# Shared rows turned on TensorE and stored as eight rows, early reloads into other places, one root for a norm of four tiles

## The chip, the cores and the metric

The kernel runs on one core of a Trainium2 chip. The metric is the device time of one execution in microseconds (us). The engines of the core are TensorE (PE, matrix products), VectorE (DVE), ScalarE (ACT), GpSimd (POOL) and SyncE (SP, which here only issues transfers); each takes its own instructions in order, and they wait for one another by semaphores. Transfers between DRAM and the on-chip memory are issued from a queue of SP or of POOL and run on 16 DMA engines.

## The reference

One layer on 1024 tokens of width 1024, all in float32:

```python
mod = silu(c) @ w_ada + b_ada
sh1, sc1, g1, sh2, sc2, g2 = split(mod, 6)
h = x * (1 + sc1) + sh1
z = h @ w_in + b_in
y = concat([y_a, y_b, y_c, y_d]) @ w_o        # four causal mixers on slices of z
x = layer_norm(ALPHA * x + (1 + g1) * y, ln1_g, ln1_b)
h = x * (1 + sc2) + sh2
f = (silu(h @ w_gate) * (h @ w_up)) @ w_down
x = layer_norm(ALPHA * x + (1 + g2) * f, ln2_g, ln2_b)
```

`mod` has six parts of 1024 numbers that are the same for every token. Two of them, `1 + g1` and `1 + g2`, multiply along the width of a tile whose rows are tokens, so each of the 128 partitions needs all 1024 numbers: a shared row.

## The kernel before

A float32 product is made of three products of pairs: `split` (L79) casts a tile to a high part on ACT (L80) and takes the low part as a difference on DVE (L81), and `passes` (L128) issues three matmuls, L130 to L132, into one PSUM bank. So every operand that PE reads has been through one ACT and one DVE instruction first.

Weights arrive through SP's queue in tiles of 128x1024, 512 KB each, in a ring of four buffers, `raw` (L71): a load waits in the queue until the tile that held its buffer has been read for the last time, and everything behind it in the queue waits too. `ada(j)` (L166) multiplies a tile of `w_ada` with the condition on DVE (L168) and so gives one column of `mod`: 128 numbers, one per partition; eight such columns are one part. There are 48 of them, spread over the first half of the program and a part of the second.

`spread` (L469) makes a shared row: it stores the eight columns to DRAM (L472) and loads the 1024 numbers back into all 128 partitions (L474). It is called twice, for `g1row`, which `res1` (L573) reads, and for `g2row`, read by `res2` (L849).

The tokens are in two halves, c = 0 and c = 1, of four tiles of 128. The program runs: input projections and mixers; the output projection of half 0, tile by tile in five steps (`first_step`, `tail`), with the y of the last mixer, the short convolution, finished on DVE in `short_out` (L877); `ln1` of half 0, which also stores the transposed h2 to DRAM; gate and up products of half 0 (`c11`); output projection and `ln1` of half 1 (`out_proj1`, `done`), interleaved with more `c11`; then the gate and up products of the other quarters after Strassen's scheme (`strassen`), for which `ln1` of half 1 makes the sum operands T1: L613 loads half 0's first four k-tiles of h2 back (`b11`), L614 subtracts, L618 stores the result; then the down-projection, also by Strassen (`dn_product`), in which each quarter's operands come by loads L810 and go through `split`. It ends with the last norms, `ln2` (L855). Half 1's norms stand in the middle of the last products, half 0's at the very end.

`ln2` works by tile: statistics of two half rows (L861, L863), their aggregate (L864), a root on POOL (`rsqrt`, L390, nine small instructions L397 to L415 for one column, twelve for four), then two passes over the row (L867, L871) and a store for each half row (L872). `ln1_[t]` is the generator of tile t of half 1; `run` advances it by one or all its steps, and the steps' places among the products set the order on DVE, as the code is written.

The order of the instructions on PE, and in parts on DVE and ACT, is that of the code (`in_order`); elsewhere a scheduler places them. An `after(a, b)` sets an issue order between two instructions.

## Time and profile before

| | |
|---|---|
| time, three runs | median 1024.22 us (1017.43 to 1025.0) |
| the profiled execution | 1024.31 us, its span 1022.5 us |
| granted TensorE clock, mean | 0.974 |
| PE busy | 960.3 us, 94% |
| DVE busy | 807.9 us, 79% |
| ACT, POOL busy | 358.0 us and 200.1 us |
| moved | 197.93 MB, mean 194 GB/s |

The span runs from the first instruction to the last. All positions in the profile are us from the span's start. The granted clock is a share of full speed: 1.00 is 2.4 GHz, 0.50 is 1.2 GHz. A bracket at the end of a timeline row tells how long the engine had been idle before that instruction, and what it waited for.

### The profile page before, as it was taken

The numbers are of one execution on the slowest core, as the hardware profiler recorded it, in microseconds if no ns is written. First come the engines' busy times: TensorE is split into PE (matmuls) and PEld (weight loads), VectorE is DVE, ScalarE is ACT, GpSimd is POOL, SyncE is SP. The second block draws the span as 40 slices with busy tenths as digits, with TensorE's granted clock in tenths as the row PEclk, the third lists the DMA queues.
The fourth block names the chain that finished last, engine by engine and source line by source line (L and its number), as shares of the span: only waits on it lengthen the run. The fifth ranks groups of instructions, "written<-read, shape, count | busy, mean of one in ns | idle before, by whom it ended". The sixth has DMA issues, their size and how long they took to land.

```text
span 1022.5 us, 12397 instructions
## 1 busy us (share of the span) xinstructions
PE 960.3 (94%) x4348; PEld 779.2 (76%) x4348; DVE 807.9 (79%) x1268; ACT 358.0 (35%) x545; POOL 200.1 (20%) x537
## 2 busy tenths in 40 slices
PE   8949999898999999988989999999999999999984
PEld 7737777676887877877768788888788877888863
DVE  5848998789669963638798888888766799898887
ACT  4532221342473353275332222222223243544230
POOL 7990000300251020352000000000000000000506
PEclk9979999999999999999999999999999999999998
DMA  8923212786554464378965554445438897655542
GB/s 310 322 99 127 58 34 71 246 206 232 177 190 175 144 224 147 128 276 265 339 238 216 196 195 168 167 180 158 163 133 272 308 308 267 216 192 176 189 150 82
DMA packets 78751, 197.93 MB, mean 194 GB/s; under 512 B 11425, under 2 KB 17601, under 8 KB 78689
## 3 DMA queue, kind: packets, MB, share of 16 engines
q1 hardware_dynamic: 67648, 157.82, 46.5%
q0 software_dynamic: 11040, 39.33, 10.6%
q8 instruction: 34, 0.56, 0.2%
q14 instruction: 29, 0.23, 0.1%
HBM read 153.79 MB, written 42.74 MB: 192 GB/s over the span
## 4 chain that ended last, share of the span: by engine, by line
PE 29%; issue 26%; DVE 11%; POOL 8%; DMA 7%; ACT 3%; SPq 0%; POOLq 0%; DVEq 0%; ACTq 0%
PE mm L132 9%; PE mm L130 9%; PE mm L131 9%; DVE pr L81 3%; DMA tmp<-in_w_down_dram 2%; DVE acc L429 1%; DMA raw<-in_w_ada_dram 1%; DVE raw L168 1%; POOL rs_b L402 1%; ACT tmp L603 1%; POOL rs_a L397 1%; DMA raw<-h_d 1%; ACT pr L80 1%; PE sm L130 1%; DMA raw<-in_w_o_dram 1%
## 5 line engine op out<-in xcount | busy, mean ns | idle before, releaser
L80 ACT CAST pr<-raw 128x1024 fp32r<-128x1024 f32 (+1 forms) x157 | 133.6, 876 | 178.5 <-PE mm L132 67.8
L81 DVE TENSOR_TENSOR pr<-raw,pr 128x1024 fp32r<-128x1024 f32 (+1 forms) x157 | 155.3, 1002 | 32.9 <-ACT pr L80 32.4
L130 PE MATMUL mm<-bop,pr 128*128 128x512 f32 x264 | 103.4, 392 | 2.5 <-DVE c L774 1.5
L132 PE MATMUL mm<-bop,pr 128*128 128x512 f32 x264 | 102.8, 389 | 0.0
L131 PE MATMUL mm<-bop,pr 128*128 128x512 f32 x264 | 102.7, 389 | 0.0
L131 PE MATMUL mm<-pr 128*128 128x512 f32 x250 | 97.9, 391 | 4.7 <-DVE pr L81 4.7
L130 PE MATMUL mm<-pr 128*128 128x512 f32 x250 | 97.4, 390 | 0.1
L132 PE MATMUL mm<-pr 128*128 128x512 f32 x250 | 97.3, 389 | 0.0
L429 DVE SCALAR_TENSOR_TENSOR acc<-up,pack,acc 128x512 f32<-128x512 f32 x120 | 84.6, 749 | 0.1
L130 PE MATMUL mm<-h,pr 128*128 128x512 f32 (+1 forms) x208 | 78.2, 376 | 6.5 <-ACT p L650 5.6
L132 PE MATMUL mm<-h,pr 128*128 128x512 f32 (+1 forms) x208 | 76.4, 367 | 2.9 <-DVE pr L81 2.9
L131 PE MATMUL mm<-h,pr 128*128 128x512 f32 (+1 forms) x208 | 76.6, 368 | 0.0
L130 PE MATMUL mm<-tb,pr 128*128 128x512 f32 x176 | 69.5, 395 | 2.9 <-DVE tmp L764 2.9
L132 PE MATMUL mm<-tb,pr 128*128 128x512 f32 x176 | 69.6, 396 | 0.7 <-DVE pr L81 0.7
L131 PE MATMUL mm<-tb,pr 128*128 128x512 f32 x176 | 69.0, 392 | 0.0
L168 DVE SCALAR_TENSOR_TENSOR raw<-raw,cond 128x1024 f32<-128x1024 f32 x48 | 58.0, 1220 | 13.2 <-DMA raw<-in_w_ada_dram 13.1
L397 POOL TENSOR_SCALAR rs_a<-lmv 128x1 f32<-128x1 f32 x16 | 9.2, 575 | 295.2 <-DVE lmv L864 179.5
L80 ACT CAST pr<-room 128x512 fp32r<-128x512 f32 x60 | 34.3, 618 | 86.8 <-PE mm L132 83.1
L130 PEld LDWEIGHTS mm<-bop,pr 128*128 128x128 f32 x264 | 49.5, 188 | 15.4 <-issue 2.1
L131 PEld LDWEIGHTS mm<-pr 128*128 128x128 f32 x250 | 46.9, 188 | 16.2 <-DVE pr L81 6.7
L132 PEld LDWEIGHTS mm<-bop,pr 128*128 128x128 f32 x264 | 49.6, 188 | 10.4
L131 PEld LDWEIGHTS mm<-bop,pr 128*128 128x128 f32 x264 | 49.6, 188 | 9.9
(337 smaller groups left out, 2153.9 us busy)
## 6 DMA issues: line engine op xcount, KB each, us to landing
raw<-in_w_ada_dram SPq DMA_DIRECT2D x48, 512.0 KB, 4.9
raw<-in_w_down_dram SPq DMA_DIRECT2D x25, 512.0 KB, 3.4
raw<-in_w_gate_dram SPq DMA_DIRECT2D x23, 512.0 KB, 4.8
raw<-in_w_up_dram SPq DMA_DIRECT2D x23, 512.0 KB, 4.3
raw<-s_d SPq DMA_DIRECT2D x20, 512.0 KB, 4.9
raw<-in_w_o_dram SPq DMA_DIRECT2D x16, 512.0 KB, 4.7
raw<-act_d SPq DMA_DIRECT2D x15, 512.0 KB, 4.1
tmp<-in_w_down_dram SPq DMA_DIRECT2D x15, 512.0 KB, 4.6
```

The lines of the kernel that those rows point to most:

```text
L80: S.copy(hi, src)
L81: V.tensor_tensor(out=lo, in0=src, in1=hi.bitcast(F32), op=SUB)
L130: PE.matmul(o, wh, xh, start=first, stop=False, skip_group_check=True)
L131: PE.matmul(o, wh, xl, start=False, stop=False, skip_group_check=True)
L132: PE.matmul(o, wl, xh, start=False, stop=last, skip_group_check=True)
L168: V.scalar_tensor_tensor(out=w, in0=w, scalar=1.0, in1=cond, op0=MUL, op1=MUL, accum_out=mod[:, j:j + 1])
L397: G.tensor_scalar(out=a, in0=v, scalar1=EPS, scalar2=None, op0=ADD)
L402: G.tensor_scalar(out=b, in0=o, scalar1=o, scalar2=a, op0=MUL, op1=MUL)
L429: V.scalar_tensor_tensor(out=o, in0=u, scalar=dww[:, i, j:j + 1], in1=o, op0=MUL, op1=ADD)
L603: S.activation(dst, src, AF.Identity, scale=hA[:, kk:kk + 1], bias=hB[:, kk:kk + 1])
```

## The change

1. `spread` turns the eight columns on PE: `PE.transpose` gives an 8x128 block in PSUM, ACT copies it into the first eight partitions of the row tile, and the store writes 8 runs of 128 numbers instead of 1024 single numbers. The call for `g1row` moves from before `ada(34)` to after `first_step(0)`.
2. `b11` gets its own places, half of the second row tile (tag "rowb") twice and the two accumulators of the convolution, and its four loads are written before `out_proj1` instead of inside `ln1`.
3. For half 1 a new generator, `ln2_all`, takes the four tiles together: all statistics, one root of 128x4, both passes on whole rows, and stores of whole rows at its end, of which the one of tile 0 is ordered behind the last load.

```diff
     def spread(col, tag):
         row_d = dr.tile([1, D], F32, name=f"{tag}_d", bufs=2)
-        SP.dma_start(row_d.rearrange("o (k p) -> (o p) k", p=P), col)
+        o = sm()
+        PE.transpose(o[:KT, :P], col, ident)
         row = yp.tile([P, D], F32, name="row", tag=tag)
+        turned = row[:KT, :P]
+        S.copy(turned, o[:KT, :P])
+        SP.dma_start(row_d.rearrange("o (k p) -> (o k) p", p=P), turned)
         SP.dma_start(row, row_d.to_broadcast([P, D]))
...
         if c == 1:
-            b11 = raw_p.tile([P, 1024], F32, name="raw", tag="raw", bufs=4)
-            bv = b11[:, :CH].rearrange("p (k t) -> p k t", k=4)
-            SP.dma_start(bv, h2_d[:4, :, t * P:(t + 1) * P].rearrange("k p t -> p k t"))
+            bv = b11[t]
             V.tensor_tensor(out=bv, in0=hv[:, :4], in1=bv, op=SUB)
...
+    def ln2_all(rr):
+        st = cst.tile([P, 4, 2, 6], F32, name="lst4")
+        mv = cst.tile([P, 4, 2], F32, name="lmv4")
+        rs = cst.tile([P, 4], F32, name="lrs4")
+        for h in (1, 0):
+            for t, r in enumerate(rr):
+                V.bn_stats(st[:, t, h], r[:, H[h]])
+            yield
+        for t in range(4):
+            V.bn_aggr(mv[:, t], st[:, t])
+        rsqrt(rs, mv[:, :, 1])
+        yield
+        for t, r in enumerate(rr):
+            V.scalar_tensor_tensor(out=r, in0=r, scalar=mv[:, t, 0:1], in1=l2g, op0=SUB, op1=MUL)
+            V.scalar_tensor_tensor(out=r, in0=r, scalar=rs[:, t:t + 1], in1=l2b, op0=MUL, op1=ADD)
+            yield
+        for t, r in enumerate(rr):
+            i = SP.dma_start(out[(4 + t) * P:(5 + t) * P], r)
+            if t == 0:
+                after(i, loaded[-1])
...
-        g1row = spread(mod[:, 16:24], "rowa")
         for j in range(34, 40):
             ada(j)
...
             first_step(n)
+            if n == 0:
+                g1row = spread(mod[:, 16:24], "rowa")
             ada(24 + 2 * n)
...
+        b11 = yp.tile([P, 2, CH], F32, name="b11", tag="rowb")
+        b11 = [b11[:, t] for t in range(2)] + [sl.tile([P, CH], F32, name="b11", tag=f"acc{i}") for i in range(2)]
+        b11 = [b.rearrange("p (k t) -> p k t", k=4) for b in b11]
+        for t in range(4):
+            SP.dma_start(b11[t], h2_d[:4, :, t * P:(t + 1) * P].rearrange("k p t -> p k t"))
         out_proj1(mid, done)
...
-            run(ln1_[t], 1)
+        run(ln1_, 1)
...
-        for t in range(2):
-            run(ln1_[t])
+        run(ln1_, 2)
...
-            if g in (1, 3):
-                run(ln1_[2 + g // 2])
+            if g < 4:
+                run(ln1_, 1)
+        run(ln1_)
```

The order on SP around the first shared row (`rowa_d` is its copy in DRAM, `row` its tile). Before:

```order
L73 DMA raw<-in_w_ada_dram 128x1024 x2
L472 DMA rowa_d<-mod 128x8x1
L73 DMA raw<-in_w_ada_dram 128x1024 x6
L474 DMA row<-rowa_d 128x1024
L73 DMA raw<-in_w_ada_dram 128x1024 x4
L73 DMA raw<-in_w_o_dram 128x1024
L73 DMA raw<-in_w_ada_dram 128x1024 x4
L73 DMA raw<-in_w_o_dram 128x1024 x5
```

With the change:

```order
L73 DMA raw<-in_w_ada_dram 128x1024 x12
L73 DMA raw<-in_w_o_dram 128x1024
L73 DMA raw<-in_w_ada_dram 128x1024 x4
L73 DMA raw<-in_w_o_dram 128x1024
L477 DMA rowa_d<-row 8x128
L73 DMA raw<-in_w_o_dram 128x1024 x2
L478 DMA row<-rowa_d 128x1024
L73 DMA raw<-in_w_o_dram 128x1024 x2
```

The store and the row load have moved behind all those w_ada loads and now stand among the five w_o loads.

On SP around `ln1` of half 1 (L613 loads `b11`, L757 belongs to the Strassen products). Before:

```order
L757 DMA p_4017<-p_d 128x1024
L613 DMA raw<-h_d 128x4x128 x2
L73 DMA raw<-in_w_gate_dram 128x1024
L73 DMA raw<-in_w_up_dram 128x1024
L613 DMA raw<-h_d 128x4x128 x2
L73 DMA raw<-in_w_gate_dram 128x1024
L73 DMA raw<-in_w_up_dram 128x1024
```

With the change, first where the loads of `b11` now stand, some 25 rows of the queue earlier (their tiles are called `b`), then the place they have left:

```order
L1065 DMA b_3281<-h_d 128x4x128
L73 DMA raw<-in_w_gate_dram 128x1024
L73 DMA raw<-in_w_up_dram 128x1024
L1065 DMA b_3281<-h_d 128x4x128
...
L1065 DMA b_3282<-h_d 128x4x128
L1065 DMA b_3283<-h_d 128x4x128
...
L759 DMA p_4019<-p_d 128x1024
L73 DMA raw<-in_w_gate_dram 128x1024
L73 DMA raw<-in_w_up_dram 128x1024
L73 DMA raw<-in_w_gate_dram 128x1024
```

The weights of the next products now follow the `p` load directly.

On DVE in the last norm of half 1, where `r` are its rows, `lmv` the means, `lrs` the roots and `pr` operands for PE. Before:

```order
L867 SCALAR_TENSOR_TENSOR r_6274<-r_6274,lmv,row 128x1024
L864 BN_AGGR lmv<-lst_7360 128x2
L871 SCALAR_TENSOR_TENSOR r_6274<-r_6274,lrs,row 128x512 x2
L81 TENSOR_TENSOR pr<-raw,pr 128x512
L867 SCALAR_TENSOR_TENSOR r_6275<-r_6275,lmv,row 128x1024
L81 TENSOR_TENSOR pr<-raw,pr 128x1024
L871 SCALAR_TENSOR_TENSOR r_6275<-r_6275,lrs,row 128x512 x2
L864 BN_AGGR lmv<-lst_7366 128x2
L867 SCALAR_TENSOR_TENSOR r_6276<-r_6276,lmv,row 128x1024
L871 SCALAR_TENSOR_TENSOR r_6276<-r_6276,lrs,row 128x512
L81 TENSOR_TENSOR pr<-raw,pr 128x1024 x2
L871 SCALAR_TENSOR_TENSOR r_6276<-r_6276,lrs,row 128x512
```

With the change:

```order
L891 SCALAR_TENSOR_TENSOR r_6279<-r_6279,lmv_7360,row 128x1024
L81 TENSOR_TENSOR pr<-raw,pr 128x1024
L81 TENSOR_TENSOR pr<-raw,pr 128x512
L892 SCALAR_TENSOR_TENSOR r_6278<-r_6278,lrs_7361,row 128x1024
L892 SCALAR_TENSOR_TENSOR r_6279<-r_6279,lrs_7361,row 128x1024
L891 SCALAR_TENSOR_TENSOR r_6280<-r_6280,lmv_7360,row 128x1024
L81 TENSOR_TENSOR pr<-raw,pr 128x512
L81 TENSOR_TENSOR pr<-raw,pr 128x1024
L892 SCALAR_TENSOR_TENSOR r_6280<-r_6280,lrs_7361,row 128x1024
L891 SCALAR_TENSOR_TENSOR r_6281<-r_6281,lmv_7360,row 128x1024
L892 SCALAR_TENSOR_TENSOR r_6281<-r_6281,lrs_7361,row 128x1024
L81 TENSOR_TENSOR pr<-raw,pr 128x1024 x2
```

The four aggregates (L887) now stand just ahead of these rows, and each reader of a root (L892, in place of L871) reads a column of the one wide root, `lrs`.

## Rows read from the trace of the kernel before

**Rows 1.** The page: busy us (share of the span) and instructions of each engine.

```profile
PE 960.3 (94%) x4348; PEld 779.2 (76%) x4348; DVE 807.9 (79%) x1268; ACT 358.0 (35%) x545; POOL 200.1 (20%) x537
```

**Rows 2.** Windows: A:B, length, busy PE, PEld, DVE, ACT, POOL, clock, DMA share, GB/s.

```profile
217.76:241.43 23.67, 20.37 (x87) 15.80 (x85) 23.67 (x47) 5.83 (x10) 0.00 (x0) 1.00 0.77 268
241.96:245.37 3.41, 3.41 (x10) 2.66 (x9) 3.41 (x5) 0.00 (x0) 0.00 (x0) 0.50 0.65 238
463.82:467.24 3.42, 3.42 (x9) 2.66 (x9) 3.29 (x6) 0.00 (x0) 0.55 (x1) 0.50 0.98 385
500.00:525.00 25.00, 21.20 (x82) 15.52 (x81) 22.62 (x37) 9.38 (x15) 2.15 (x4) 0.94 0.97 365
```

**Rows 3.** PE's timeline: start, length, line, operands; in brackets idle time before, releaser.

```profile
241.49 0.50 PE L130 MATMUL mm<-pr,ys 128*128 128x512 f32 x1 [3.20 <-DVE y L877]
463.07 0.50 PE L130 MATMUL mm<-h,pr 128*128 128x512 f32 x1 [2.72 <-ACT p L650]
717.99 0.47 PE L130 MATMUL mm<-tb,pr 128*128 128x512 f32 x1 [0.69 <-DVE tmp L764]
976.15 0.50 PE L131 MATMUL mm<-pr 128*128 128x512 f32 x1 [2.15 <-DVE pr L81]
990.04 0.50 PE L131 MATMUL mm<-pr 128*128 128x512 f32 x1 [0.94 <-DVE pr L81]
993.56 0.40 PE L130 MATMUL mm<-pr 128*128 128x512 f32 x1
```

**Rows 4.** DVE's timeline, same columns.

```profile
217.76 1.23 DVE L168 SCALAR_TENSOR_TENSOR raw<-raw,cond 128x1024 f32<-128x1024 f32 x1 [3.67 <-DMA raw<-in_w_ada_dram]
456.17 0.69 DVE L614 TENSOR_TENSOR raw<-tmp,raw 128x512 f32<-128x512 f32 x1 [8.58 <-DMA raw<-h_d]
806.30 1.23 DVE L1091 TENSOR_TENSOR keep<-tmp 128x1024 f32<-128x1024 f32 x1 [5.62 <-DMA tmp<-in_w_down_dram]
809.18 0.69 DVE L1088 TENSOR_SCALAR keep<-keep 128x1024 f32<-128x1024 f32 x1
974.21 0.75 DVE L871 SCALAR_TENSOR_TENSOR r<-r,lrs,row 128x512 f32<-128x512 f32 x1 [2.73 <-POOL lrs L415]
974.88 2.35 DVE L81 TENSOR_TENSOR pr<-raw,pr 128x1024 fp32r<-128x1024 f32 x2
995.98 0.67 DVE L1132 TENSOR_TENSOR f<-mm,row 128x512 f32<-128x512 f32 x1
```

**Rows 5.** SP's queue: start of issuing, time from first to last issue, transfer, count.

```profile
203.44 0.38 SPq L472 DMA_DIRECT2D rowa_d<-mod  x1
204.75 16.46 SPq L73 DMA_DIRECT2D raw<-in_w_ada_dram  x6
244.34 6.64 SPq L73 DMA_DIRECT2D raw<-in_w_o_dram  x5
451.63 1.37 SPq L613 DMA_DIRECT2D raw<-h_d  x2
800.72 0.50 SPq L1087 DMA_DIRECT2D keep<-in_ln_b_row_dram  x1
```

**Rows 6.** The page, transfers: count, size, median us from issue to landing.

```profile
raw<-in_w_ada_dram SPq DMA_DIRECT2D x48, 512.0 KB, 4.9
```

**Rows 7.** The row stores of L472, both.

```profile
DMA to landing us min/median/max: 8.9/9.7/10.5
```

**Rows 8.** The loads of b11, L613, all four.

```profile
DMA to landing us min/median/max: 2.9/3.8/4.7
```

**Rows 9.** POOL's timeline: a wide root, the t_d store, one instruction of a small root.

```profile
365.23 1.10 POOL L397 TENSOR_SCALAR rs_a<-cmv 128x4 f32<-128x4 f32 x1 [0.87 <-DVE cmv L451]
369.26 0.20 POOL L415 TENSOR_TENSOR crs<-crs,rs_b 128x4 f32<-128x4 f32 x1
446.19 0.76 POOL L618 DMA_DIRECT2D t_d<-raw  x1
958.51 1.17 POOL L402 TENSOR_SCALAR rs_b<-lrs,rs_a 128x1 f32<-128x1 f32 x1
```

More of the change, by code (lines that the diff above doesn't have):

```diff
@@ L799, in strassen @@
         G.dma_start(s_d[j, 1].rearrange("p a t -> p (a t)"), hi[1])
+    loaded = []
     GR = tuple((j, min(j + 2, FT // 2)) for j in range(0, FT // 2, 2))
@@ L809, in rows @@
             t = raw_p.tile([P, 1024], F32, name="raw", tag="raw", bufs=4)
-        SP.dma_start(t[:, :n * CH].rearrange("p (j t) -> p j t", j=n),
-                     src.rearrange("j p t -> p j t")[:, GR[g][0]:GR[g][1], H[q]])
+        loaded.append(SP.dma_start(t[:, :n * CH].rearrange("p (j t) -> p j t", j=n),
+                                   src.rearrange("j p t -> p j t")[:, GR[g][0]:GR[g][1], H[q]]))
         return t[:, :n * CH]
@@ L1105, in trunk @@
             S.copy(r0[t][:, H[0]], oA[t])
-        ln0, ln1_ = [[ln2(c, t, (r0, r1)[c][t]) for t in range(4)] for c in range(2)]
+        ln0, ln1_ = [ln2(0, t, r0[t]) for t in range(4)], ln2_all(r1)
         dn_product(oB, lambda g: sum_rows(g, 0, 0), kept, True, False)
```

## The prediction

> **What bounds the kernel now.** First the share of each engine: TensorE (PE) is busy 960.3 of 1022.5 us and VectorE (DVE) 807.9 [rows 1]. PE works in order and is nearly full, so only two things can make the time shorter: its idle gaps, and the stretches in which the granted clock falls to 0.50 (the 1.2 GHz level). In such a stretch of 3.41 us PE does half its work, so each costs 1.7 us; two of them, from 241.96 and 463.82, begin just behind a PE gap [rows 2]. So I went on to the PE timeline and took the gaps that stand at places of the change, with what ended them: 3.20 us at 241.49, 2.72 at 463.07, 0.69 at 717.99, 2.15 at 976.15 and 0.94 at 990.04 [rows 3]. For each I followed the releaser back through the timelines of DVE, POOL and SP's queue. The reader should see that each chain ends in an operation that the change moves or removes.
>
> **Gap at 241.49: the first shared row.** PE waits for L877 on DVE, the end of work that DVE does without a pause from 217.76 to 241.43: 23.67 us busy of 23.67 [rows 2]. At 217.76 DVE had been idle for 3.67 us, waiting for a w_ada load [rows 4]. SP issued that load at 204.75, right behind the 4-byte store L472 of 203.44 [rows 5]: 13.0 us to landing, where such a load takes 4.9 [rows 6]. The store took 8.9 to 10.5 us itself [rows 7], 1024 elements of 4 bytes in one transfer. I read the late load as the store's doing. Without that store there the load would land near 209, DVE's 3.67 us of waiting go, and L877 is done before PE needs it: the gap's 3.20 us and the 1.7 of low clock behind it go, 4.9 in all. Against it: one more PE instruction (the transpose, 8 output rows of 128; the nearest rows are matmuls of 512 columns that take 0.40 to 0.50, so 0 to 0.5, I take 0.3 with its switch of operands), and SP's new waits. Store and row load now stand between the w_o loads: the store waits for ACT's copy, which is queued behind a w_o cast, and the row load waits for the store to land; behind it are two w_o loads, x loads and w_gate. In before the five w_o loads were issued from 244.34 to 250.98 [rows 5]. With the gap gone the first of them is at 240.3, its cast ends some 5 us later, the store goes near 246, and with a landing of x us the last two w_o loads are issued at 246 + x: no later than before if x is up to 5. For x I take the nearest transfer in runs of 512 bytes, L613, with 2.9 to 4.7 us [rows 8]; I give 0.6 for the loads that slip against the earlier PE. So 4.9 − 0.3 − 0.6 = **4.0**. Ends: 4.9 if both costs vanish; −1.5 if the new SP wait makes a stall as large as the old one (the gap of 3.2 comes back, and 1.2 for the rest of its chain and the transpose).
>
> **Gap at 463.07: b11.** PE waits for ACT's copies of p, ACT and DVE having been held up by L614, which starts at 456.17 after 8.58 us of waiting for the b11 load [rows 4]. SP issued that load at 451.63 [rows 5]: b11 lives in the ring of four `raw` tiles, and its slot had to wait for the store to t_d that POOL issued at 446.19 [rows 9]. In the change these four loads stand before out_proj1 and go into tiles of their own (the second row tile and the two convolution accumulators), so this wait has no place left; w_gate and w_up loads that were queued behind it move ahead too. The gap's 2.72 and the low clock's 1.7 go: **4.4**. Do the early loads block SP? The first waits for tile rowb (last read by a w_o cast), the third and fourth for the accumulators; in the order w_gate, w_up and two w_o loads stand behind them, each needed long after. I price that at 0; its cover is the four loads already in the ring. Ends: 2.7 (the low clock merely comes elsewhere) and 7.1 (the earlier weights also remove a later gap of the same 2.7).
>
> **Gap at 717.99 and the start of the down-projection.** The second row store is issued shortly before 717.99 and an activation load behind it is late; PE loses 0.69 [rows 3]. It moves to the end of the strassen part: **0.7** (0 to 0.7). Its new place is near 798, between loads of w_down. There the first w_down load no longer stands behind the row load, for which DVE now waits 5.62 us at 806.30, a gain for DVE; but the row load and the ln_b row behind it (issued 800.72, read by DVE at 809.18 [rows 4, 5]) wait for the store to land. Store 798.8, ln_b issued x + 0.7 later, 4.9 to landing: 809.2 is met up to x of about 5. I take **0**; ends −4 (a stall that eats the slack DVE has here) and +1.6.
>
> **Gaps at 976.15 and 990.04: the last norm.** In before DVE asks for four roots one after the other and idles for each; the fourth time 2.73 us, to 974.21, and the L81 of PE's operand (its cast long done) stands right behind, at 974.88 [rows 4]. PE waits 2.15, then 0.94. In the change one root serves four tiles, and in DVE's order only two instructions of the norm and two L81 stand between its statistics and the first use. Alone the 4-wide root takes 365.23 to 369.46 = 4.2 us [rows 9]. On the clock of before, the last statistics would be done near 956.5 (an estimate: the first root was asked for shortly before, and four statistics go in a row), the root at about 961. Behind it the order has six norm instructions, of whole rows (1.4, an estimate from the 0.75 of L871's half row), and two L81 (1.9 together) up to the L81 that PE waited for: 961 + 6 × 1.4 + 1.9 is 971.3, that L81 ends 1.2 later, and PE's gap began at 976.15 − 2.15 = 974.0. So 2.15 + 0.94 = 3.1 go. The end of the kernel is PE's last tiles followed by DVE's norm of the first half: PE gets tile 0 ready at 993.96 while DVE takes it up at 995.98 without idling [rows 3, 4]. DVE is behind by 2.0 there, and with the root waits gone it can catch up by as much; I take 1.2. **4.3**, ends 2 (only the larger gap) and 5.5. Whole-row stores hide behind this: they are SP's, and only the store of tile 0 is last.
>
> **Sum.** 4.0 + 4.4 + 0.7 + 0 + 4.3 = 13.4. The profiled run took 1024.31 (span 1022.5), the median of the runs is 1024.22, so the same base serves: 1024.3 − 13.4 = **1010.9**, say 1011. All upper ends together give 1002.
>
> **Rivals.** *Given back.* From 500 to 525 the transfers are at a share of 0.97 [rows 2]; a PE that is 8 us early there meets loads that cannot come 8 us early, and the 4.4 of b11 is lost: 1015. Or the SP wait eats the 4.0 of the first row: also 1015. Both: 1019. For it speak that share and the two w_o loads behind the row load; against it that the weights behind b11 are now issued some 5 us earlier (near 446.2 and not after 451.6).
>
> *The root under load.* A POOL operation of the small root took 1.17 us beside a busy DVE (at 958.51), against 0.20 for the last one of the wide root with DVE free [rows 9]. If all 12 operations take 1.17, the root ends 14.0 after its start near 954, at 968, DVE's later norm pushes L81 some 10 us back, to 978: PE waits about 5.5 and loses 1.7 of clock. In place of +4.3 that is −5.1: 1020.3. Against it: too few DVE instructions stand ahead of the root's first reader to go on colliding for 14 us; DVE then idles and POOL runs free. The Trainium skill, page "SBUF — State Buffer", section "Who interferes with whom", says that DVE and GpSimd share one pair of ports under an exclusive lock; by that rule this rival is what happens as long as DVE has instructions with two SBUF operands. The 1.17 beside the 0.20 agrees with it, but does not show how long it lasts here.
>
> *Slower.* The store's landing is set by its queue and by DRAM, not by its 1024 pieces: x stays at 8.9 to 10.5. Then two w_o loads and the ln_b row are late by x − 5 each, and each stall brings low clock: 2(x − 5) + 3.4. At 10.5 that is 14.4 against 13.4 won: 1025.3. It decides from x = 10.0; at the median of 9.7 it ends at 1023.7. For it: all L472 stores shown took that long, under different load. Against: a transfer in 512-byte runs lands in 2.9 to 4.7 [rows 7, 8]. The Trainium skill, page "DMA: Bandwidth & Descriptors", section "Anatomy of one DMA — SWDGE (gpsimd) path", gives about 2 us fixed per transfer, most of it the write receipt, and the rest by bytes; by that, an estimate, x would be 2 and the first row worth about 0.4 more. No row shows a small row store.
>
> *Not what it says.* Of the four stores said to go last, three still stand among the loads and wait for DVE, as all did before. If they hold the last operand loads as the old ones did, the 3.1 of this stage stays: 1014.
>
> **How the numbers follow.** The forecast with its own range of 1004 to 1015 gets 0.60; given back (1015 to 1019) 0.28; root under load 0.05; stores not last 0.02; slower 0.05. 1011 is the likeliest. The range of 1004 to 1020 leaves out the last two rivals above it and the sum of all upper ends, some 0.15. A measurement of this kernel tells about 1%, 10 us, from no change: faster than 1014 is the forecast but for its upper edge, 0.55; within 1% is all the rest but an unforeseen stall, 0.43; slower 0.02, since even the slower rival stays within 1%.
>
> **What would show it.** Right: no PE gap of over 1 us between 235 and 245 and between 455 and 470, no low clock behind them; the w_ada load near 204 landing in about 5; the new store landing in under 5; no DVE wait before L614; one DVE wait of at most 4 us for the wide root, and no PE gap ended by L81 from 965 to 985. Wrong: PE gaps ended by w_o casts after 240; longer gaps between 490 and 525; POOL operations of over 1 us through the whole root; DVE waiting for the ln_b row after 800. The forecast fails first if DVE before 241 has another wait behind the load, since its chain has no idle time to absorb one.

## The result and the profile after

The changed kernel takes 1009.5 us (median; 1008.06 to 1012.4) beside 1024.61 for the kernel before, a ratio of 0.9873 with a 95% interval of 0.9845 to 0.9902: 13.0 us less, between 10.0 and 15.9. A second series of both kernels gave 0.9868 (0.984 to 0.9896). The forecast was 1011 with a range of 1004 to 1020.

The profiled execution took 1012.4 us, its span 1010.6. The page's first part, which answers to [rows 1] (busy us, share, instructions):

```profile
PE 949.5 (94%) x4350; PEld 771.2 (76%) x4350; DVE 807.3 (80%) x1264; ACT 358.5 (35%) x547; POOL 189.2 (19%) x513
```

PE is busy 10.8 us less, although it issues two instructions more. Its idle time (span less busy) has gone from 62.2 to 61.1 only. So in this pair of executions nearly the whole gain stands in the granted clock, not in the gaps: between 195 and 990 us before had eight stretches of 3.41 us at 0.50, after two. Where the gaps went is seen in PE's timeline of after, which answers to [rows 3] (start, length, line, operands; in brackets the idle time before and what ended it):

```profile
256.79 0.50 PE L131 MATMUL mm<-pr,ys 128*128 128x512 f32 x1 [0.67 <-DVE pr L81]
285.77 0.39 PE L132 MATMUL mm<-h,pr 128*128 128x256 f32 x1 [2.04 <-DVE pr L81]
295.05 0.33 PE L597 MATMUL mm<-ident,r 128*128 128x128 f32 x1 [1.11 <-ACT r L587]
439.13 0.50 PE L130 MATMUL mm<-h,pr 128*128 128x512 f32 x1 [2.89 <-ACT p L652]
452.67 0.50 PE L130 MATMUL mm<-h,pr 128*128 128x512 f32 x1 [1.47 <-ACT p L652]
468.09 0.47 PE L130 MATMUL mm<-tb,pr 128*128 128x512 f32 x1 [1.19 <-DVE tmp L766]
490.88 0.47 PE L130 MATMUL mm<-bop,pr 128*128 128x512 f32 x1 [3.50 <-ACT bop L80]
836.29 0.50 PE L130 MATMUL mm<-pr 128*128 128x512 f32 x1 [0.70 <-ACT pr L80]
837.56 0.50 PE L131 MATMUL mm<-pr 128*128 128x512 f32 x1 [0.77 <-DVE pr L81]
```

The gaps of 3.20, 0.69, 2.15 and 0.94 us are gone; the one of 2.72 is 1.47. Those of 2.04 and 2.89 stood in before too. New are 0.67 at 256.79, 1.11 at 295.05, 1.19 at 468.09 and, above all, 3.50 at 490.88, in a stage that the change hardly touches.

Both kernels issue the same 4348 matmuls in the same order (the change adds two between them). So the time between two given matmuls can be set side by side. This table, worked out from the PE timelines, has one row for each profiled execution of this study, which is one for each kernel and two for the changed one, and six stretches (us; the positions are those of before): the first shared row (in before from 235.0 to 260.5), b11 (447.7 to 478.8), the operands T2 to T4 (478.8 to 521.4), the end of the Strassen products with the gap near 718 (714.9 to 817.8), the start of the down-projection (817.8 to 861.2), and the last part of PE (970.0 to 1007.6).

```
kernel                          row    b11   T2-4  near718  down   last
before                         25.5   31.1   42.6   103.0   43.3   37.6
b11 alone                      23.4   28.0   43.9   104.9   45.2   37.4
last norm alone                25.5   31.0   44.6   104.7   43.1   33.3
rows alone                     20.8   31.2   43.2   102.1   48.1   37.3
old store in the changed       23.2   27.6   45.7   105.9   43.7   33.3
changed                        21.1   28.4   46.0   102.2   44.5   33.3
changed, second execution      20.4   27.8   44.7   102.2   44.4   33.3
first row at the old place     20.2   28.0   44.6   102.2   44.3   33.3
T1 kept                        20.3   26.6   45.5   102.1   44.2   33.3
T1 kept, two b21 early         20.5   26.9   44.3   102.1   45.6   33.3
T1 and T2 kept                 20.3   27.7   46.2   102.2   44.2   33.3
the same, row at old place     20.2   25.6   46.0   102.2   45.5   33.3
T1, half of T2 kept            20.5   26.2   42.9   102.3   45.2   33.3
the same, row at old place     20.4   25.5   43.2   102.1   42.8   33.3
```

Every stretch has two groups of kernels, with and without the part of the change that bears on it, and the means of the groups give what each part is worth: first row 24.4 to 20.5 (3.9 us won), b11 31.1 to 28.0 (3.1 won; kernels that keep T1 left out), T2 to T4 43.5 to 45.0 (1.5 lost), near 718 104.6 to 102.2 (2.4 won), start of the down-projection 43.8 to 44.9 (1.1 lost), last 37.4 to 33.3 (4.1 won). Together 10.9 us of the 13.0.

In the four stretches that won, no kernel of one group lies among the other group. In the two that lost, the groups overlap: 42.6 to 44.6 against 43.9 to 46.0, and 43.1 to 45.2 against 42.8 to 48.1. By the same timelines PE's waiting between T2 and T4 rose from 5.2 to 5.9 us on the mean, 0.7 of the 1.5; the time at a clock of 0.50 rose there from 1.2 to 3.5 us, and that is the rest. In the down-projection 0.5 us is waiting. So both losses hold a part that may be chance.

**Why the first gap went.** In SP's queue of after, the new store and the row load behind it, both times (start of issuing, time to the last issue, transfer, count):

```profile
241.54 0.34 SPq L477 DMA_DIRECT2D rowa_d<-row  x1
242.27 2.93 SPq L73 DMA_DIRECT2D raw<-in_w_o_dram  x2
245.31 0.37 SPq L478 DMA_DIRECT2D row<-rowa_d  x1
...
789.15 0.29 SPq L477 DMA_DIRECT2D rowa_d<-row  x1
791.91 0.81 SPq L478 DMA_DIRECT2D row<-rowa_d  x1
```

The row load waits for the store to land and goes out 3.8 and 2.8 us behind it, so the store lands in less than that; in before it took 8.9 to 10.5 [rows 7]. The w_ada loads issued between 203 and 209, three in before and two in after, landed in:

```profile
DMA to landing us min/median/max: 11.8/12.5/13.0
```

```profile
DMA to landing us min/median/max: 4.4/4.4/4.4
```

And the windows of 12 us around them, before and then after (A:B, length, busy PE, PEld, DVE, ACT, POOL, clock, DMA share, GB/s):

```profile
204.00:216.00 12.00, 12.00 (x40) 7.48 (x39) 9.41 (x16) 7.38 (x10) 0.00 (x0) 0.98 0.77 45
```

```profile
207.00:219.00 12.00, 12.00 (x43) 7.77 (x42) 11.32 (x24) 5.94 (x8) 0.00 (x0) 1.00 0.64 193
```

And the packets, in before from 203 to 215 and in after from 207 to 217:

```profile
DMA packets 1118, 0.32 MB, mean 27 GB/s; under 512 B 1040, under 2 KB 1040, under 8 KB 1118
```

```profile
DMA packets 492, 1.82 MB, mean 182 GB/s; under 512 B 48, under 2 KB 48, under 8 KB 492
```

With the 4-byte store in flight the DMA engines are busy 77% of the time and move 45 GB/s; without it 64% and 193 GB/s. Nearly all packets of that time, 1040 of 1118, are the small ones. The store of 4 KB holds back loads of 512 KB.

**The last norm.** POOL's root in after, which answers to [rows 9], the first reader of the root on DVE, and the L81 for which PE waited in before:

```profile
946.47 1.15 POOL L397 TENSOR_SCALAR rs_a<-lmv 128x4 f32<-128x4 f32 x1 [156.12 <-DVE lmv L887]
949.99 0.52 POOL L405 TENSOR_TENSOR rs_b<-rs_b,rs_a 128x4 f32<-128x4 f32 x1
950.60 0.19 POOL L407 TENSOR_SCALAR rs_c<-rs_b 128x4 f32<-128x4 f32 x1
952.59 0.20 POOL L415 TENSOR_TENSOR lrs<-lrs,rs_b 128x4 f32<-128x4 f32 x1
```

```profile
952.83 2.48 DVE L892 SCALAR_TENSOR_TENSOR r<-r,lrs,row 128x1024 f32<-128x1024 f32 x2 [2.38 <-POOL lrs L415]
961.87 2.35 DVE L81 TENSOR_TENSOR pr<-raw,pr 128x1024 fp32r<-128x1024 f32 x2
```

The root took 6.3 us in all. Its first instructions are slow while DVE works, and from the moment DVE has come to its wait (950.5) each takes 0.2. DVE waits 2.38 us once, where it waited four times, 7.5 us in all.

### The profile page after: what moved, and what is told of

Its sections match the earlier page's. It is cut to its first block, busy times and chain, and to the rows that moved or that the text cites. A ratio compares the mean times of both kernels' runs of the same rounds, so it can differ in the third digit from the quotient of the medians.

```text
span 1010.6 us, 12362 instructions
## 1 busy us (share of the span) xinstructions
PE 949.5 (94%) x4350; PEld 771.2 (76%) x4350; DVE 807.3 (80%) x1264; ACT 358.5 (35%) x547; POOL 189.2 (19%) x513
## 3 DMA queue, kind: packets, MB, share of 16 engines
q0 software_dynamic: 11040, 39.33, 10.5%
## 4 chain that ended last, share of the span: by engine, by line
issue 31%; PE 19%; DVE 13%; POOL 8%; DMA 8%; ACT 4%; SPq 0%; POOLq 0%; DVEq 0%; ACTq 0%
PE mm L132 6%; PE mm L131 6%; PE mm L130 6%; DVE pr L81 3%; DVE raw L168 2%; DMA tmp<-in_w_down_dram 2%; DVE acc L429 2%; DMA raw<-in_w_o_dram 1%; DMA raw<-h_d 1%; ACT tmp L607 1%; POOL rs_b L402 1%; DMA raw<-in_w_up_dram 1%; POOL rs_a L397 1%; DMA keep<-in_ln_g_row_dram 1%; DMA t_d<-raw 1%
## 5 line engine op out<-in xcount | busy, mean ns | idle before, releaser
L81 DVE TENSOR_TENSOR pr<-raw,pr 128x1024 fp32r<-128x1024 f32 (+1 forms) x157 | 155.2, 1001 | 33.8 <-ACT pr L80 33.3
L130 PE MATMUL mm<-h,pr 128*128 128x512 f32 (+1 forms) x208 | 75.7, 364 | 5.3 <-ACT p L652 4.4
L132 PE MATMUL mm<-h,pr 128*128 128x512 f32 (+1 forms) x208 | 74.4, 358 | 2.9 <-DVE pr L81 2.9
L131 PE MATMUL mm<-h,pr 128*128 128x512 f32 (+1 forms) x208 | 74.2, 357 | 0.0
L397 POOL TENSOR_SCALAR rs_a<-lmv 128x1 f32<-128x1 f32 (+1 forms) x13 | 7.3, 565 | 298.8 <-DVE lmv L887 156.1
L132 PEld LDWEIGHTS mm<-bop,pr 128*128 128x128 f32 x264 | 49.6, 188 | 10.4
```

What stands on the lines that cost most here:

```text
L81: V.tensor_tensor(out=lo, in0=src, in1=hi.bitcast(F32), op=SUB)
L130: PE.matmul(o, wh, xh, start=first, stop=False, skip_group_check=True)
L131: PE.matmul(o, wh, xl, start=False, stop=False, skip_group_check=True)
L132: PE.matmul(o, wl, xh, start=False, stop=last, skip_group_check=True)
L397: G.tensor_scalar(out=a, in0=v, scalar1=EPS, scalar2=None, op0=ADD)
```

## The experiments

**The three parts alone.** Each kernel is before with the lines of one part of the change, all of them and no other. The edits are shown in part; `...` marks a cut. Rows alone:

```diff
-        SP.dma_start(row_d.rearrange("o (k p) -> (o p) k", p=P), col)
+        o = sm()
+        PE.transpose(o[:KT, :P], col, ident)
         row = yp.tile([P, D], F32, name="row", tag=tag)
+        turned = row[:KT, :P]
+        S.copy(turned, o[:KT, :P])
+        SP.dma_start(row_d.rearrange("o (k p) -> (o k) p", p=P), turned)
...
-        g1row = spread(mod[:, 16:24], "rowa")
...
+            if n == 0:
+                g1row = spread(mod[:, 16:24], "rowa")
```

> Only the first part of the change is in: rows turned on PE, stored as eight rows, the first call moved; b11 and the last norm as before. By the traces of before and after, aligned on PE's instructions, PE had won 3.95 us between 235 and 262 and 0.7 at 718, and lost 1.0 between 797 and 851. Theory A (each part keeps its own gaps): 1024.3 - 3.95 - 0.7 + 1.0, about 1020.7, and the granted clock falls behind the gaps near 289, 317, 388 and 447 as in before. Theory B (the clock's stretches at 0.50 near 289, 317, 388 and 447 were lost with the first gap, because PE runs on without one): these four go here too, worth 1.7 each less 1.1 for a new gap near 295, so about 1015. Theory C (the stretches come and go from one execution to the next): they are neither all there nor all gone, and the runs of one kernel scatter by some us.

Measured: 1016.94 us, ratio 0.9947 (0.9925 to 0.9969), so 5.4 us less (3.2 to 7.7). That holds theory A's 3.6 and leaves out theory B's 9. Its profiled execution, 1023.8 us, was the slowest of its ten; it lost 4.8 us at the start of the down-projection, far more than any other. Of theory B's four low stretches two were gone (near 289 and 317), two were there (384 and 442), which is what theory C says.

b11 alone:

```diff
-            SP.dma_start(bv, h2_d[:4, :, t * P:(t + 1) * P].rearrange("k p t -> p k t"))
+            bv = b11[t]
...
+        b11 = yp.tile([P, 2, CH], F32, name="b11", tag="rowb")
...
+        for t in range(4):
+            SP.dma_start(b11[t], h2_d[:4, :, t * P:(t + 1) * P].rearrange("k p t -> p k t"))
```

> Only the second part is in: the four loads of b11 early, in places of their own. Theory A (the gap near 463 and the clock behind it go, and nothing comes back): 1024.3 - 4.4, about 1020. Rival (given back in the stage after it): the gap near 463 goes, but new waits for loads of h2 on PE between 465 and 500 take 3 to 4.5 back, as in the trace of after (3.50 at 490.88): 1023 to 1025. By theory C on the clock the stretches at 0.50 near 289, 317 and 388, which lie ahead of anything that this part changes, differ from before's by chance; by theory B they are as in before.

Measured: 1021.75 us, ratio 0.9986 (0.9962 to 1.001): no difference that can be told. The stretch of b11 is 3.1 us shorter than in before, the one behind it 1.3 longer, and the gap near 718 stood at 2.65 in this execution. Theory A's 4.4 lies outside the interval: alone this part brings at most 3.9 us, more likely about 1.4. The rival's time fits, but of the 3 to 4.5 us that it wanted back between 465 and 500 the stretch shows 1.3.

The last norm alone:

```diff
-        ln0, ln1_ = [[ln2(c, t, (r0, r1)[c][t]) for t in range(4)] for c in range(2)]
+        ln0, ln1_ = [ln2(0, t, r0[t]) for t in range(4)], ln2_all(r1)
...
```

> Only the third part is in: one root for the four tiles of half 1's last norm, whole rows, the new order of the stores. Theory A: the gaps of 2.15 and 0.94 go and 1.0 of smaller ones, as in after: 1024.3 - 4.1, about 1020. Rival (these gaps had gone in after only because PE and DVE came there in another relation): half of it or less, 1022 or more. The stretches of low clock ahead of 900 should be those of before, since nothing ahead of it is touched; if they differ, they come by chance.

Measured: 1018.87 us, ratio 0.9965 (0.9939 to 0.9992), 3.6 us less. The last stretch takes 33.3 us, the same to 0.1 us as in every kernel with this part. Theory A holds. The three parts alone, 5.4, 1.4 and 3.6, make 10.4 of the 13.0, which their intervals allow. Ahead of 900, where this kernel is that of before, the low stretch near 388 was absent and one near 502 was new: by what was expected, chance.

**The changed kernel once more**, for its clock.

> The changed kernel itself, unaltered, for another profiled execution and more runs. Theory C (the stretches at 0.50 of the clock behind gaps come in one execution and not in the next): the profile shows the same PE gaps within 0.5 us, above all 2.0 near 286, 2.9 near 439, 3.5 near 491 and 2.3 near 513, but another set of low stretches between 200 and 1000 us than the two of the first execution (near 202 and 513), rather four to six. Theory B (the change took the gaps' low clock away): again no low stretch near 286, 314, 382 and 439. Median by both 1008 to 1012.

Measured: 1011.1 us (1007.07 to 1015.71). The gaps near 284 and 437 were the same within 0.1 us, but not all: those of 1.47 and 1.19 were absent, and in place of 3.50 for ACT stood 2.98 at 491.37 for a sum of DVE. The windows behind the same gap of 2.0 us, in the changed kernel near 286, in this second execution near 284, and in the kernel with T1 kept, which has the same instructions up to there, near 286 (columns as above):

```profile
285.77:289.18 3.41, 3.41 (x28) 3.33 (x29) 1.92 (x4) 3.38 (x5) 2.50 (x5) 1.00 0.88 335
439.13:442.54 3.41, 3.41 (x15) 2.83 (x16) 1.31 (x2) 3.41 (x8) 2.27 (x4) 1.00 0.96 273
```

```profile
283.64:287.05 3.41, 3.41 (x28) 3.33 (x29) 1.92 (x4) 3.38 (x5) 2.50 (x5) 1.00 0.88 336
437.29:440.70 3.41, 3.41 (x8) 2.73 (x9) 1.32 (x2) 3.41 (x8) 2.27 (x4) 0.50 0.98 279
```

```profile
285.74:289.15 3.41, 3.41 (x18) 3.41 (x18) 1.39 (x3) 2.92 (x5) 2.32 (x7) 0.50 0.92 370
```

The same gap, 2.03 to 2.04 us, was followed by full clock twice and by half clock once, and the 2.89 us gap near 438 by full clock in one execution of the changed kernel and half in the other. Over all fourteen executions the gap of 2.0 us was followed by a fall to 0.50 seven times. Between 262 and 450 us the four kernels with the old row store had 4, 3, 3 and 4 low stretches, the ten with the new one 0, 2, 2, 4, 2, 4, 3, 0, 1 and 0. So theory C holds for the single execution; whether the lower mean (1.8 against 3.5) is the change's doing or chance is open. Between the same matmuls from 260.5 to 447.7 the four take 186.6 us on the mean and the ten 184.5: 2.1 less, which is what the stretches of the table leave of the 13.0. Not every low stretch costs 1.7 us. The part from 280 to 305 took 25.0 us in before, with the low stretch near 289, and 24.7 in after, without it, since PE then waits 1.11 us at 295.05; the part from 305 to 330 took 25.2 and 23.5.

**The old store in the changed kernel**, and the new store at the old place.

```diff
# old store
-        o = sm()
-        PE.transpose(o[:KT, :P], col, ident)
...
+        SP.dma_start(row_d.rearrange("o (k p) -> (o p) k", p=P), col)
# old place
         for j in range(32, 34):
             ada(j)
+        g1row = spread(mod[:, 16:24], "rowa")
...
-            if n == 0:
-                g1row = spread(mod[:, 16:24], "rowa")
```

> The changed kernel with the old store of a shared row, 1024 pieces of 4 bytes taken from the columns, without transpose and copy; the call for the first row stands where the change put it, but in SP's order the store, which waits for nothing late now, comes four w_ada loads earlier than its place in the change, with four w_ada loads and the row load behind it. Theory F (the form of the store counts: whatever stands behind 1024 small pieces is late): the w_ada load behind it takes over 10 us again, the PE gap near 239 is back with 2 to 3.5 us, the store in the second half is again early and the gap near 715 back with 0.7 to 2.6; 4 to 5 us slower than the changed kernel, 1013 to 1016. Rival (the place counts): no gap, within 1 us of the changed kernel.

Measured: 1017.14 us, ratio 0.9935 (0.9902 to 0.9967), 6.0 us above the changed kernel of the same series, 1.0 more than theory F expected at most. SP's queue, the landing of its two row stores, that of the three w_ada loads issued between 203 and 209, and DVE's and PE's waits:

```profile
206.82 0.43 SPq L472 DMA_DIRECT2D rowa_d<-mod  x1
208.26 9.13 SPq L73 DMA_DIRECT2D raw<-in_w_ada_dram  x4
```

```profile
DMA to landing us min/median/max: 10.3/10.8/11.3
```

```profile
DMA to landing us min/median/max: 3.2/8.2/11.7
```

```profile
220.04 1.23 DVE L168 SCALAR_TENSOR_TENSOR raw<-raw,cond 128x1024 f32<-128x1024 f32 x1 [3.00 <-DMA raw<-in_w_ada_dram]
```

```profile
240.88 0.50 PE L130 MATMUL mm<-pr,ys 128*128 128x512 f32 x1 [2.70 <-DVE y L898]
716.83 0.47 PE L130 MATMUL mm<-tb,pr 128*128 128x512 f32 x1 [2.00 <-DVE tmp L762]
```

The longest, 11.7 us, is the load right behind the store, at 208.26; the 8.2 us are of the load just ahead of it. Theory F holds: both gaps are back with the form of the store, at another place in the queue than in before. For the first row no kernel here has the old store later than 207 or the new one earlier than 235; that the form does it, and not the time of issue, rests on the packets above and on the new store's short landing.

> The changed kernel with the first row's call at its old place, before ada(34), but turned on PE and stored as eight rows. In SP's order the store now stands behind fifteen w_ada loads and one w_o load, with one w_ada load between it and the row load, and all five w_o loads are behind both. Theory F: no gap near 239, since the store takes 2.5 to 4; the wait of the row load moves ahead of the w_o loads, so 0 to 3 us of delay for them: 1009 to 1013. Rival (the place counts, because PE turns the columns only when it comes by and SP waits for it): a gap of 3 us or more between 235 and 262, 1013 or more.

Measured: 1009.74 us, ratio 0.9844 (0.9815 to 0.9874). No gap between 235 and 262; that stretch takes 20.2. PE turns the columns in time, SP's store stands behind fifteen w_ada loads and not ahead of them, and the rival's wait doesn't arise: the place of the call is worth under 1 us of that stretch.

**What gives time back near 490.** Four edits of that stage, each with the changed kernel as its base. First, T1 kept on the chip:

```diff
# T1 kept
-            G.dma_start(t1_d[:, :, tt].rearrange("k p t -> p k t"), bv)
...
-            t1, b22 = load(a[:, H[0]], t1_d[k]), load(a[:, H[1]], h2_d[4 + k][:, CH:])
-            V.tensor_tensor(out=t1, in0=b22, in1=t1, op=SUB)
+            t1, b22 = a[:, H[0]], load(a[:, H[1]], h2_d[4 + k][:, CH:])
+            for t in range(4):
+                ts = slice(t * P, (t + 1) * P)
+                V.tensor_tensor(out=t1[:, ts], in0=b22[:, ts], in1=b11[t][:, k], op=SUB)
```

Then, beside this edit, two of T4's operands early; all of T2 in the place of T1; or half of it:

```diff
# two b21 early
+        b21s = [yp.tile([P, 2, CH], F32, name="b21", tag="rowb")]
+        b21s = [b21s[0][:, t] for t in range(2)]
+        for k in range(2):
+            load(b21s[k], h2_d[4 + k][:, :CH])
...
# all of T2 kept
-            G.dma_start(t2_d[k], t1)
...
+            for ts, t1 in t1_parts(k):
...
+                V.tensor_tensor(out=t1, in0=x, in1=t1, op=SUB)
...
# half of T2 kept: k = 0, 1 in the second row's place
+        for k in (2, 3, 0, 1):
...
+            if k > 1:
+                G.dma_start(t2_d[k], a[:, H[0]])
```

> The changed kernel with one thing more: T1 stays on the chip. The differences that L620 stored to DRAM and the next stage loaded again (four stores and four loads of 256 KB) are read from the places of b11 itself; the subtraction of 128x512 becomes four of 128x128. Theory G (the stage from 460 to 500 gives the won time back because its operands come through DRAM, at a DMA share near 1): without 2 MB of it, some 5.7 us of transfers at the 362 GB/s of that stage, the gaps of 1.19 at 468 and 3.50 at 490.88 shrink, 2 to 4.5 us: 1005 to 1008 beside 1009.5. Rival (the chain that waits there is that of T2's stores and the reloads behind them, not of T1): less than 1 us. Rival (twelve more small DVE instructions delay the casts): 1010 or more.

Measured: 1012.8 us (1006.8 to 1013.97), ratio 0.9899 (0.9854 to 0.9944). The gaps of 1.47, 1.19 and 3.50 are gone, the stretch of b11 is 1.4 shorter; but 3.51 us of waiting stand at 496, for DVE, and the stretch of T2 to T4 is 45.5. Theory G falls. The time lies where the second rival (more small instructions on DVE) put it, but its interval overlaps the changed kernel's, and the next kernel has the same instructions and took 1009.34; the runs don't tell the two rivals apart.

> The kernel with T1 kept on the chip, and two of the four b21 operands of T4 loaded into the place of the first half of b11 ahead of T3's loads, not through the ring behind them. Theory G2 (what stops PE near 496 with T1 kept, 3.51 us, is T4's loads, queued behind T3's in the ring): the gap shrinks to under 2, T4's subtractions come earlier, and the kernel is 1 to 3 us faster than with T1 kept alone, about 1008. Rival (the transfers are at their limit there, a DMA share of 0.96 to 0.99, so an operand that comes earlier makes another one late): the gap goes elsewhere between 470 and 520 and the time is that of T1 kept, 1010 to 1013.

Measured: 1009.34 us, ratio 0.9855 (0.9826 to 0.9885). The waits are 2.21 at 489.64, 1.48 at 496.84 and 3.16 at 511.70: moved, not gone. PE's waiting in the stretch is 7.1 us beside 6.2 with T1 kept, as the rival has it. The median is 3.5 below that of T1 kept, where theory G2 wanted 1 to 3, but the two intervals overlap, and T1 kept had 4.5 us at a clock of 0.50 in this stretch, this kernel none.

> The changed kernel with T1 and T2 both kept in the places of b11: T2 is subtracted in place and cast from there, so the ring tile of T2 is free as soon as it is subtracted, and neither T1 nor T2 is stored and loaded again (eight stores and eight loads of 256 KB less); each subtraction and split of T2 becomes three smaller ones. Theory H (what gives the won time back is SP's wait for T2's stores to land, 7.8 us in the changed kernel, before T3's and T4's loads can use the ring again): the gaps of PE between 465 and 500 (1.2 to 3.5, 5.6 to 8.7 idle in the stretch that ends with the gap near 513) shrink by 3 or more, and that stretch, 45.0 us on the mean of the kernels with early b11, goes to 41 or less; 1004 to 1007. Rival (the transfers of the next weights limit it): the stretch stays above 43.5, 1009 or more.

> The kernel that keeps T1 and T2, with the first row's call at its old place as well. By the theory that the place of the call is worth little (the stretch from 235 to 262 was 20.2 against 20.4 to 21.1 us), within 1 us of the kernel before it in this list; if both are worth what they seem (1 us and 4 us), 1003 to 1006, the fastest of all. Rival: 1009 or more, if keeping T2 brings nothing.

Measured: 1010.03 us, ratio 0.9845 (0.9817 to 0.9873), and 1008.2 us, 0.9842 (0.9816 to 0.9867). Theory H falls in this form: SP no longer waits for T2's stores, and yet the stretch is 46. Between the two kernels, which differ in the place of the first row's call, the ratios are the same to 0.0003. The one gap that is left, in the second of these kernels, and DVE just ahead of it:

```profile
491.39 0.76 PE L130 MATMUL mm<-bop,pr 128*128 128x512 f32 x1 [8.01 <-DVE c L784]
```

```profile
488.62 0.83 DVE L715 TENSOR_TENSOR raw<-raw,b 128x256 f32<-128x256 f32 x3
489.36 1.28 DVE L778 TENSOR_TENSOR c<-p,mm 128x512 f32<-128x512 f32 x2
490.56 1.28 DVE L784 TENSOR_TENSOR c<-c,mm 128x512 f32<-128x512 f32 x2
```

L778 writes c12, which in the first Strassen product lives in the accumulators, and there the edit had kept T2 until its last reader, L715. The experiment made a wait of its own. The next one avoids it:

> T1 kept on the chip, and of T2 only the first two operands, in the second row's place; the other two go through DRAM as before but are made first, so their stores start earlier, and the accumulators come free as soon as T2 is subtracted. The two kernels that kept all of T2 held the accumulators until T4, and c12 of the first Strassen product lives there: its first sum came only at 489, right behind T4's last subtraction, and PE stood for 7 to 8 us. Theory H2 (with that conflict gone the shorter way of T2 shows): no PE gap over 2 us between 470 and 505, the stretch that ends with the gap near 513 takes 41 us or less in place of 44 to 46, 1004 to 1008. Rival (DVE and the next weights' transfers set the stretch, whatever T2 does): the stretch stays at 43.5 or more, 1008 to 1012.

> The same with the first row's call at its old place, before ada(34). By H2 and a place worth under 1 us: 1003 to 1007, the fastest of all, ratio to the kernel before under 0.984. By the rival 1008 or more, ratio 0.985 or above.

Measured: 1008.17 us, ratio 0.9856 (0.9827 to 0.9884), and 1009.74 us, 0.986 (0.9826 to 0.9894). Both times lie where the rival put them. The gap of 8 is gone and no gap over 2 us stands between 470 and 505, but 3.17 us stand near 506 to 509, for DVE's first sum of the next product: the gap of 2.23 to 2.27 that before and the changed kernel have there, grown by 0.9. The stretch takes 42.9 and 43.2: 2 us less than the 45.0 that kernels with early b11 take, half of what H2 wanted. But PE's waiting in it, 5.8 and 5.5 us, is hardly under their mean of 5.9; what is missing is the clock at 0.50, none here and 3.5 us on their mean. So that T2's shorter way shortened the stretch is not shown. The windows of this stretch, before, changed, and half of T2 kept:

```profile
478.77:521.41 42.64, 37.98 (x160) 29.30 (x159) 36.56 (x59) 18.41 (x31) 5.17 (x10) 1.00 0.94 337
```

```profile
468.09:514.09 46.00, 38.47 (x159) 29.74 (x160) 37.82 (x61) 18.67 (x31) 5.39 (x10) 0.99 0.88 319
```

```profile
466.94:509.88 42.94, 37.15 (x160) 29.53 (x159) 36.56 (x64) 17.99 (x31) 4.20 (x8) 1.00 0.84 296
```

In all three PE needs about 37 to 38 us, DVE about 37 and the transfers 0.84 to 0.94 of the time. Each of the three is in use for 82 to 94% of the stretch, and in these runs what was taken from one wait turned up, in the main, at the next. What of the three is the last bound isn't settled; an order on DVE with c12's sums ahead of T4's subtractions wasn't tried. None of the seven variants that were meant to be as fast or faster (these six and the row at its old place) is told apart from the changed kernel by its interval.

## Why the prediction was right

The time, 1009.5, lies 1.5 us below the forecast. The mechanism was right at the first row, at the last norm and in the half clock behind the gap of b11; but that the sum came within 0.4 us of the 13.0 is in part luck, since the terms that were not right made up for each other. One sum was wrong: all upper ends together, 4.9, 7.1, 0.7, 1.6 and 5.5, are 19.8 and give 1004.5, not 1002, which is inside the range and not below it. And two of its signs of being right failed: a gap of 1.19 us stands between 455 and 470, and DVE still waits ahead of the successor of L614, L616, for ACT now:

```profile
449.65 0.69 DVE L616 TENSOR_TENSOR b<-tmp,b 128x512 f32<-128x512 f32 x1 [3.65 <-ACT tmp L607]
```

The terms one by one:

- *First row, 4.0.* Right in size and cause: 3.9 on the means, 4.4 in the two profiled executions (25.5 to 21.1). The old store was what made the w_ada load late, as the return of the gap with the old store shows. The 0.6 for loads that slip is the 0.67 us gap at 256.79, in this execution; it was 0.38 with rows alone and absent in the changed kernel's second. The 1.7 of low clock in the sum was not certain: two of the four kernels with that gap didn't have it.
- *b11, 4.4.* Too large. The stretch won 3.1: of the gap's 2.72 us 1.47 stay here, and 1.17, 0.84, 0.66 and nothing in the four other executions with b11 early and T1 stored, since ACT's copies of p are late for another reason, which the wait for b11 had hidden. ACT's timeline of after:

```profile
448.11 2.90 ACT L607 ACTIVATE tmp<-mm,hB,hA 128x128 f32<-128x128 f32 x8 [2.99 <-DMA h_d<-tmp]
```

  L607 waits 2.99 us for its target, whose store of h2 isn't done. In all five executions with b11 early and T1 stored it waits so, 2.99 to 4.16 us; in the six kernels that keep T1 on the chip this wait is gone, and the gap with it. So the stores of T1 belong to the cause. The low clock behind the gap, 1.7 of the term, was present in the three kernels without the early loads and absent in those five. Then 1.5 are lost between 468 and 514, 0.7 of it in waiting. That was the rival "given back": right in its place, and a third of its 4.4. Alone this part is not told from nothing.
- *Gap near 718, 0.7.* Mis-sized, from one execution: 0.69 there, but 2.65, 2.46 and 2.00 in three others with the old store. The stretch won 2.4, above the end of 0.7 that was set. A wait behind a slow transfer should have had a range of the size of that transfer's own spread.
- *Start of the down-projection, 0.* Within its ends: 1.1 lost on the mean, in groups that overlap. DVE's wait of 5.62 [rows 4] became two, of 1.68 for w_down and 3.17 for the ln_g row.
- *Last norm, 4.3.* Right in the sum, 4.1, but not in its parts: in before the gaps, 3.2 with a small one of 0.13, and slower matmuls right behind them were all of it, and the 1.2 of catching up at the end of DVE weren't there. From the start of PE's last matmul to the end of the span it is 14.9 us in both executions.
- *Not in the sum.* The low stretches near 289, 317, 388 and 447, none of which the prediction touched, were absent from the profiled execution of after. From 260.5 to 447.7 it was 4.3 us shorter than before, which nearly made up for the b11 term in that pair (2.7 won, 3.4 lost between T2 and T4).

The root's rival was right in its mechanism and wrong in its length: 1.06 to 1.15 us for each of the first three instructions beside DVE, 0.2 once DVE waits, 6.3 in all where it gave 14.0 and the forecast 4.2. (It also let the root start at 954, ahead of the statistics that the forecast has done at 956.5.) The Trainium skill, page "SBUF — State Buffer", section "Who interferes with whom", has DVE and GpSimd under an exclusive lock on a shared port pair; the trace agrees for as long as DVE has work, 4.0 us here. The rival "slower" fell with the landing of the new store, below 3.8 and 2.8 us where it needed 10. The Trainium skill, page "DMA: Bandwidth & Descriptors", section "Anatomy of one DMA — SWDGE (gpsimd) path", gave 2, but for the path of POOL's queue, while SP issues this store; no row shows the landing itself, only these bounds. And "not what it says" fell with the last stretch: no gap is left in it, with three stores still among the loads.

## What to carry to other kernels

A store of a few KB in 4-byte pieces costs more than its own landing: here it held back the loads that were in flight with it, so turn such data on the chip first; here that cost one transpose of 0.27 us and one copy of 0.26 us for each row. A gap that is closed ahead of a stage in which two or three resources are nearly full may not bring its whole length, so value it by the time between the same two matmuls, the second of them behind that stage. And take what the clock costs from several executions and from lengths: one profile has its low stretches by chance, and one of them cost 0.3 us, another 1.6.

## What the runs showed of the hardware

A transfer of 4 KB in 1024 pieces kept the DMA engines 77% busy for about 10 us at 45 GB/s, and the 512 KB loads behind it landed in 11.8 to 13.0 us, where two at the same place took 4.4 without it. With the store put elsewhere by the edit of the old store, the load just ahead of it took 8.2 us and the one behind 11.7. The Trainium skill, page "DMA: Bandwidth & Descriptors", section "Why small descriptors are slow (HBM only)", has a fixed cost per packet as the reason for slow small pieces, which agrees; that other loads pay for it is what the rows add. And after nearly equal idle times of PE at the same place, 2.03 to 2.05 us, the granted clock fell to 0.50 in seven executions and stayed at 1.00 in seven, and one gap of 2.65 us (near 715, b11 alone) was followed by no fall at all.
